# A hybrid encoder layer on one core: how the group norms, the mixer's table splits and the gate products are put in order

## The chip, the cores and the metric

The kernel runs on one core of one Trainium2 chip. The metric is the device time of one execution in microseconds (us). Engines: PE (TensorE, matmuls; its weight loads are shown as PEld), DVE (VectorE), ACT (ScalarE), POOL (GpSimd), and SP, which here only issues DMAs. Every engine works through its own queue in a fixed order that is set when the kernel is built; engines wait for each other by semaphores.

## The reference: what is computed

One encoder layer over 512 tokens of 1024 channels, in float32, batch 1:

- n = RMSNorm(x). z = n W_in with W_in 1024x2048, cut into four parts of 512 channels: `x_lru`, `g_lru`, `a_glu`, `b_glu`.
- Recurrent half: a causal-like convolution of 4 taps over `x_lru`, two gated linear recurrences (forward and backward; gates by block-diagonal 64x64 matrices and sigmoids), their sum times gelu(`g_lru`).
- Convolution half: `a_glu` x sigmoid(`b_glu`), a depthwise convolution of 31 taps, a layer norm over groups of 64 channels, SiLU.
- Both halves are RMS-normed, joined and projected by W_out (1024x1024); h = x + that.
- PEER: queries RMSNorm(h) W_q; for each token and 8 heads the best 16 of 128x128 experts by product keys (two rankings of 128, then a ranking of sums), a softmax over the 16 as gates; each expert is a row of `peer_u` and a row of `peer_v`: out = sum of gate x gelu(u . n) x v. h = h + out, and a last RMSNorm.

## The kernel before

Matmul operands are split into a high and a low part in a rounded format (`split`: the cast to `w_hi` on ACT, L108, and the subtraction to `w_lo` on an engine given by the caller, L110); each product is three matmuls (high x high, high x low, low x high). Activations have their parts in `m_hi` and `m_lo`.

The program runs through five stages: the mixer (0 to 276 us), ranking with the queries (to about 500), the scatter of the gates into a table in memory, `scr_g` (to about 670), then the dense experts: for tokens 0 to 383 all 128 tiles of 128 experts are computed densely, while the last 128 tokens gather their rows by indirect DMA (`gather_steps`, L691 and L701 on DVE); and a short end.

*The mixer.* Four token blocks are normed (`normed`: Square on ACT L130, `rstd_of` with a Sqrt at L120, L132 on DVE) and transposed (`turn`, L140 to L142). Then a loop goes over the 16 column blocks of W_in in the order `order`; n is the turn, eb the block. A turn splits its own block (subtraction on POOL), issues the load of the block two turns ahead, and runs 24 matmuls of 512 columns (L329 to L331) into a bank `pz`. What a turn hangs on to that: a gelu, a sigmoid or the gated product; the 31-tap convolutions `convs` (of channel groups 1 and 2 on DVE, L228; of groups 0 and 3 the first 8 taps on ACT and POOL, L220 and L221, and the other 23 as matmuls with diagonal tables, `taps`, L242 to L244, whose tables are split on POOL too); the recurrences `recur(0)` at n = 9 and `recur(2)` at n = 11 (gate matmuls L265 and L267, activations L270 to L280, products and scans on DVE L285 to L294, and L288, t = 1 - t, on ACT).

The group norm of channel group j is `gnorm(j)`: a matmul for the means (L304), subtraction (L305, DVE), Square (L307, ACT), a matmul per token block for the variances (L310), `rstd_of` (five small DVE instructions and a Sqrt), transposes (L314), a copy (L316, ACT), a matmul that spreads the factors (L318), the product (L319, DVE), SiLU (L320, ACT). `gnorm(1)` is called whole in turn n = 10. After the loop come the rest of the diagonal taps of group 3, `gnorm(0)`, `gnorm(2)`, `halves(0)`, `gnorm(3)`, `project(0)` and `project(1)`. `halves(hf)` makes the two parts of four channel groups and the RMS factor `ry` of that half (Squares L389, sums on POOL L391, a matmul L400); `project(hf)` multiplies by W_out (L417 to L419) into the three `pz` banks, eight groups of 12 matmuls, and a bank is emptied by a DVE instruction that needs `ry` (L420).

*The dense experts.* `dense_u(i)` gives tile i the gelu of its scores in a buffer w (24 matmuls of 384 columns, L464 to L466); 51 tiles are made ahead (`AHEAD_U`). `weigh(i, w)` multiplies by the gates (L730, DVE), casts (L732, ACT) and subtracts (L734, DVE); `dense_v` runs 18 matmuls of 512 columns into `po` (L758). The gates come from `scr_g` in groups of 8 tiles, 1.5 MB a load (`load_gates`, L726), into two buffers `g_s`. Turn i of the last loop weighs tile i + 2 and multiplies tile i.

*What sets the order.* The framework orders each engine's instructions when the kernel is built, by the order of the program text as priority and by a model of when operands are ready; an instruction whose operands the model has ready can be put ahead of older ones. `with tc.issue_after(ins)` keeps the instructions of the block that run on the engine of `ins` behind `ins` in that engine's queue; it adds no semaphore.

Of the kernel before, what the change touches and what calls it, by code (L numbers as in the profile page):

```python
# [8 lines left out]
F32 = mybir.dt.float32  # L9
# [4 lines left out]
AF = mybir.ActivationFunctionType  # L14
ALU = mybir.AluOpType
# [3 lines left out]
P = 128  # L19
# [41 lines left out]
def tile_kernel(ctx, tc, x, par, wi, bd, kd, mg, wo, wq, keys, u_rows, v_rows, u_t, v_t, fg, ffg, sel, out):  # L61
    nc = tc.nc
# [35 lines left out]
    def f(t):  # L98
        return t.bitcast(F32)

    def load(src):
        t = raw.tile([P, D], F32, name="raw_t")
        nc.sync.dma_start(t, src)
        return t

    def split(t, eng, pool=wp):
        hi = pool.tile([P, D], F32R, name="w_hi")
        nc.scalar.copy(hi, t)  # L108
        lo = pool.tile([P, D], F32R, name="w_lo")
        eng.tensor_sub(lo, t, f(hi))  # L110
        return hi, lo

    def flat(t):
        return t.rearrange("p a b -> p (a b)")

    def rstd_of(pool, ss, n, tags=("r_v", "r_s", "r_r", "r_q")):

        v, s, r, q = (pool.tile(list(ss.shape), F32, name=t) for t in tags)
        nc.vector.tensor_scalar(v, ss, 1.0 / n, EPS, op0=ALU.mult, op1=ALU.add)
        nc.scalar.activation(s, v, AF.Sqrt)  # L120
        nc.vector.reciprocal(r, s)
        nc.vector.tensor_mul(q, r, r)
        nc.vector.tensor_mul(q, q, v)
        nc.vector.tensor_scalar(q, q, -0.5, 1.5, op0=ALU.mult, op1=ALU.add)
        nc.vector.tensor_mul(r, r, q)
        return r
# [18 lines left out]
    with ExitStack() as mx:  # L145
# [11 lines left out]
        with ExitStack() as m1:  # L157
# [8 lines left out]
            xc = a2.tile([P, 4, T], F32, name="xc", bufs=1)  # L166
            xls = [a2.tile([P, T + 3], F32, name=f"xl{i}", bufs=1) for i in range(2)]

            xt = [load(x[b * P:(b + 1) * P, :]) for b in range(2)]
            mgb = a2.tile([P, D], F32, name="mgb", bufs=1)  # L170
            nc.sync.dma_start(mgb, mg.partition_broadcast(P))
            xt += [load(x[b * P:(b + 1) * P, :]) for b in range(2, NB)]
            wts = {eb: load(wi[eb].rearrange("p c e -> p (c e)")) for eb in order[:AHEAD]}
            nc.sync.dma_start(pr, par)
            nc.sync.dma_start(sl, sel)
            nc.sync.dma_start(flat(bdt.rearrange("p a b c d -> p (a b c) d")), bd)
            nc.sync.dma_start(ffb, ffg.partition_broadcast(P))
            for xl in xls:
                nc.vector.memset(xl[:, 0:2], 0.0)
                nc.vector.memset(xl[:, T + 2:T + 3], 0.0)  # L180
# [72 lines left out]
            def advance(g, n):  # L253
                for _ in range(n):
                    next(g, None)
# [3 lines left out]
            def recur(j0):  # L259

                rs_, is_, ts_, qs_ = {}, {}, {}, {}
                for j in (j0, j0 + 1):
                    for d in range(2):
                        g_r = ps_t.tile([P, T], F32, name="pt")
                        nc.tensor.matmul(g_r, bdt[:, d, 0, j, :], xc[:, j, :], start=True, stop=True)  # L265
                        g_i = ps_t.tile([P, T], F32, name="pt")
                        nc.tensor.matmul(g_i, bdt[:, d, 1, j, :], xc[:, j, :], start=True, stop=True)  # L267
                        q = d * 4 + j
                        r = rs_[q] = a2.tile([P, T], F32, name="r")
                        nc.scalar.activation(r, g_r, AF.Sigmoid, bias=pc("brg", q))  # L270
                        ig = is_[q] = a2.tile([P, T], F32, name="ig")
                        nc.scalar.activation(ig, g_i, AF.Sigmoid, bias=pc("big", q))
                        t = ts_[q] = a2.tile([P, T], F32, name="t")
                        nc.scalar.activation(t, r, AF.Tanh, scale=lm[:, q:q + 1])
                        nc.gpsimd.tensor_mul(ig, ig, xc[:, j, :])
                for q, r in rs_.items():
                    nc.scalar.activation(r, r, AF.Exp, scale=lm2[:, q:q + 1])
                for q, t in ts_.items():
                    s = qs_[q] = a2.tile([P, T], F32, name="sq")
                    nc.scalar.activation(s, t, AF.Sqrt)  # L280
                for j in (j0, j0 + 1):
                    for d in range(2):
                        q = d * 4 + j
                        e, t, s = rs_[q], ts_[q], qs_[q]
                        nc.vector.scalar_tensor_tensor(t, e, 1.0, t, op0=ALU.add, op1=ALU.mult)  # L285
                        nc.vector.scalar_tensor_tensor(s, e, 1.0, s, op0=ALU.add, op1=ALU.mult)
                        nc.vector.tensor_mul(s, s, is_[q])
                        nc.scalar.activation(t, t, AF.Copy, scale=-1.0, bias=1.0)  # L288
                        if d == 0:
                            nc.vector.tensor_tensor_scan(hs[:, j, :], t, s, 0.0, op0=ALU.mult, op1=ALU.add)  # L290
                        else:
                            nc.vector.tensor_tensor_scan(e[:, ::-1], t[:, ::-1], s[:, ::-1], 0.0,
                                                         op0=ALU.mult, op1=ALU.add)
                            nc.vector.tensor_add(hs[:, j, :], hs[:, j, :], e)  # L294
# [3 lines left out]
            selg = sl[:, P:P + 2]  # L298
            bcg = sl[0:2, P + 2:SELN]

            def gnorm(j):
                cv = y[:, 4 + j, :]
                pb = ps_t.tile([P, T], F32, name="pt")
                nc.tensor.matmul(pb, ones64, cv, start=True, stop=True)  # L304
                nc.vector.scalar_tensor_tensor(cv, pb, -1.0 / 64.0, cv, op0=ALU.mult, op1=ALU.add)  # L305
                s = tmp.tile([P, T], F32, name="s2", bufs=3)
                nc.scalar.activation(s, cv, AF.Square)  # L307
                pv = ps_t.tile([P, T], F32, name="pt")
                for b in range(NB):
                    nc.tensor.matmul(pv[:, 2 * b:2 * b + 2], s[:, b * P:(b + 1) * P], selg, start=(b == 0), stop=(b == NB - 1))  # L310
                r = rstd_of(tmp, pv[:, 0:2 * NB], 64, ("g_v", "g_s", "g_r", "g_q"))
                pr_ = ps_t.tile([P, T], F32, name="pt")
                for b in range(NB):
                    nc.tensor.transpose(pr_[0:2, b * P:(b + 1) * P], r[:, 2 * b:2 * b + 2], ident)  # L314
                rs = tmp.tile([2, T], F32, name="rs", bufs=2)
                nc.scalar.copy(rs, pr_[0:2, :])  # L316
                pb = ps_t.tile([P, T], F32, name="pt")
                nc.tensor.matmul(pb, bcg, rs, start=True, stop=True)  # L318
                nc.vector.tensor_mul(cv, cv, pb)  # L319
                nc.scalar.activation(cv, cv, AF.Silu, scale=pc("ng", j), bias=pc("nb", j))  # L320

            for n, eb in enumerate(order):
                hi, lo = split(wts.pop(eb), nc.gpsimd)
                if n + AHEAD < len(order):
                    wts[order[n + AHEAD]] = load(wi[order[n + AHEAD]].rearrange("p c e -> p (c e)"))
                pz = ps_z.tile([P, T], F32, name="pz")
                for c in range(NC):
                    cs = slice(c * P, (c + 1) * P)
                    nc.tensor.matmul(pz, hi[:, cs], m_hi[:, c, :], start=(c == 0), stop=False)  # L329
                    nc.tensor.matmul(pz, hi[:, cs], m_lo[:, c, :], start=False, stop=False)  # L330
                    z_end = nc.tensor.matmul(pz, lo[:, cs], m_hi[:, c, :], start=False, stop=(c == NC - 1))  # L331
                kind, j = divmod(eb, 4)
                if kind == 0:
                    xl = xls[j % 2]
# [24 lines left out]
                if 1 <= n <= 4:  # L359
                    advance(convs[1], 8)  # L360
                if n >= 5:
                    advance(convs[2], {5: 7}.get(n, 4) if n < 10 or n > 12 else 0)
                if n >= 6:
                    advance(convs[0], 2)
                if n >= 12:
# [2 lines left out]
                    advance(taps[0], 1)  # L368
                if kind == 1:
                    nc.vector.tensor_mul(hs[:, j, :], hs[:, j, :], gg[:, j, :])  # L370
                if n == 10:
                    with tc.issue_after(z_end.ins):
                        gnorm(1)

            m2 = mx.enter_context(ExitStack())
            wp2 = m2.enter_context(tc.tile_pool(name="wp2", bufs=4))
# [52 lines left out]
            with tc.issue_after(z_end.ins):  # L429
                advance(taps[1], 100)  # L430
                for g in convs:
                    advance(g, 100)
                gnorm(0)
                gnorm(2)
                ry = halves(0)
                gnorm(3)
                project(0, ry)
                project(1, halves(1))
            m2.close()
# [280 lines left out]
    def gates_of(i):  # L720
        n, o = divmod(i, GQ)
        return gbuf[n][:, :, o * GT:(o + 1) * GT]

    def load_gates(n):
        t = gq.tile([P, NT, GQ * GT], F32, name="g_s")
        nc.sync.dma_start(t, scr_g[:, :, n * GQ * GT:(n + 1) * GQ * GT].rearrange("a p s -> p a s"))  # L726
        gbuf[n] = t

    def weigh(i, w):
        nc.vector.tensor_mul(w, w, gates_of(i))  # L730
        whi = gq.tile([P, TD], F32R, name="wt_hi", bufs=LAST)
        nc.scalar.copy(whi, flat(w))  # L732
        wlo = gq.tile([P, TD], F32R, name="wt_lo", bufs=LAST)
        return whi, wlo, nc.vector.tensor_sub(wlo, flat(w), f(whi))  # L734

    gq = ctx.enter_context(tc.tile_pool(name="gq", bufs=2, side="right"))
    acc = gq.tile([P, D], F32, name="acc", bufs=1)
# [136 lines left out]
```

## Time and profile before

| | |
|---|---|
| median of 3 runs | 1566.47 us (1563.59 to 1568.61) |
| the profiled execution | 1564.53 us, its span 1562.8 us |
| PE busy | 94% of the span |
| DVE busy | 79% |
| ACT busy | 41% |
| POOL busy | 42% |
| mean granted PE clock | 0.97 |
| memory traffic | 229 GB/s over the span |

PE's share counts a matmul as busy from its start to a modelled end, and consecutive matmuls overlap; so 100% of a stretch can still hold a slower pace, and the number of matmuls in a stretch says more. The granted clock is 1.0 at 2.4 GHz and 0.5 at 1.2 GHz. Idle time of an engine costs only where the chain of waits runs through it.

### The profile page before, as it was taken

The page shows a single profiled execution, that of the slowest core. Times are in us where ns is not written, and L with a number is a line of the kernel's source. Part 1 is how long each engine was busy: PE and PEld are TensorE (multiplying, and loading weights), DVE is VectorE, ACT ScalarE, POOL GpSimd, SP SyncE. Part 2 cuts the span into 40 slices and gives each one's busy share as a digit, 9 for nine tenths or more (in the row PEclk, how much of TensorE's full clock was granted, in tenths as well). Part 3 has the DMA queues.
Part 4 walks back from the last instruction along what each step waited for, and adds up shares of the span by engine and source line. Part 5 has one row for each costly group of instructions (what it writes and reads, how often), then busy time and mean ns, then how long its engine had stood idle before and what let it go on. Part 6 is the DMA issues. An engine that isn't in the chain of part 4 may idle for free.

```text
span 1562.8 us, 21636 instructions
## 1 busy us (share of the span) xinstructions
PE 1475.6 (94%) x7939; PEld 1294.8 (83%) x7939; DVE 1230.5 (79%) x2255; ACT 636.4 (41%) x937; POOL 653.0 (42%) x382
## 2 busy tenths in 40 slices
PE   5987889999988999999899999999999999999997
PEld 4764657899977889898799999999999999888886
DVE  6995745599999999948777787777777877777776
ACT  5458443344434554442233333333333333333333
POOL 3644722476551000144455555445444444444440
PEclk9998879999989999999899999999999999999999
DMA  6220412323223666589999899998989988777783
GB/s 235 87 75 14 174 42 96 114 101 103 88 96 113 224 209 230 209 254 368 334 325 344 295 340 302 334 325 301 347 300 345 320 308 308 284 276 275 263 290 134
DMA packets 137787, 358.69 MB, mean 230 GB/s; under 512 B 10064, under 2 KB 59472, under 8 KB 134352
## 3 DMA queue, kind: packets, MB, share of 16 engines
q1 hardware_dynamic: 100240, 222.03, 41.8%
q0 software_dynamic: 36864, 134.23, 23.4%
q8 instruction: 62, 1.02, 0.3%
q10 hardware_dynamic: 576, 1.05, 0.2%
q14 instruction: 45, 0.37, 0.1%
HBM read 327.91 MB, written 29.36 MB: 229 GB/s over the span
## 4 chain that ended last, share of the span: by engine, by line
PE 77%; DVE 15%; DMA 3%; ACT 2%; issue 2%; POOL 1%; SPq 0%; DVEq 0%; ACTq 0%; POOLq 0%
PE po L758 32%; PE p_e L464 10%; PE p_e L466 10%; PE p_e L465 10%; PE p_g L657 3%; DVE oa L651 2%; DMA g_s<-scr_g 2%; PE pq L573 2%; PE pq L575 2%; PE pq L574 2%; DVE w_lo L110 1%; DVE hot L647 1%; DVE pc L228 1%; PE pz L417 1%; PE pz L331 1%
## 5 line engine op out<-in xcount | busy, mean ns | idle before, releaser
L108 ACT CAST w_hi<-raw_t 128x1024 fp32r<-128x1024 f32 x302 | 316.0, 1050 | 399.0 <-PE p_e L465 255.1
L464 PE MATMUL p_e<-m_hi,w_hi 128*128 128x384 f32 x1024 | 352.6, 344 | 6.5 <-ACT w_e L473 5.7
L466 PE MATMUL p_e<-m_hi,w_lo 128*128 128x384 f32 x1024 | 349.8, 342 | 6.5 <-DVE w_lo L110 6.4
L465 PE MATMUL p_e<-m_lo,w_hi 128*128 128x384 f32 x1024 | 348.6, 340 | 0.3 <-DVE m_lo L142 0.3
L110 POOL TENSOR_TENSOR w_lo<-raw_t,w_hi 128x1024 fp32r<-128x1024 f32 x74 | 199.0, 2703 | 344.3 <-ACT w_hi L108 331.2
L679 POOL DMA_INDIRECT g_t<-in_u_rows,eidx x128 | 210.7, 1646 | 215.4 <-DVE g_t L691 175.3
L110 DVE TENSOR_TENSOR w_lo<-raw_t,w_hi 128x1024 fp32r<-128x1024 f32 x228 | 275.3, 1219 | 12.0 <-ACT w_hi L108 11.9
L679 POOL DMA_INDIRECT g_t<-in_v_rows,eidx x128 | 189.3, 1479 | 224.8 <-DVE acc L701 213.4
L758 PE MATMUL po<-w_hi,wt_hi 128*128 128x512 f32 x768 | 240.6, 393 | 0.0
L758 PE MATMUL po<-w_hi,wt_lo 128*128 128x512 f32 x768 | 239.4, 391 | 0.0
L758 PE MATMUL po<-w_lo,wt_hi 128*128 128x512 f32 x768 | 238.8, 390 | 0.0
L464 PEld LDWEIGHTS p_e<-m_hi,w_hi 128*128 128x128 f32 x1024 | 196.3, 192 | 10.9 <-ACT w_e L473 6.4
L466 PEld LDWEIGHTS p_e<-m_hi,w_lo 128*128 128x128 f32 x1024 | 195.8, 191 | 7.9 <-DVE w_lo L110 7.9
L465 PEld LDWEIGHTS p_e<-m_lo,w_hi 128*128 128x128 f32 x1024 | 195.9, 191 | 3.5 <-DVE m_lo L142 0.5
L758 PEld LDWEIGHTS po<-w_lo,wt_hi 128*128 128x128 f32 x768 | 144.1, 188 | 33.3 <-DVE w_lo L110 0.3
L758 PEld LDWEIGHTS po<-w_hi,wt_lo 128*128 128x128 f32 x768 | 144.3, 188 | 30.4
L691 DVE SCALAR_TENSOR_TENSOR g_t<-g_t,Xg 128x1024 f32<-128x1024 f32 x128 | 151.8, 1222 | 17.2 <-DMA g_t<-in_u_rows,eidx 17.2
L758 PEld LDWEIGHTS po<-w_hi,wt_hi 128*128 128x128 f32 x768 | 143.1, 188 | 25.0 <-ACT w_hi L108 0.2
L701 DVE SCALAR_TENSOR_TENSOR acc<-g_t,dots,acc 128x1024 f32<-128x1024 f32 x127 | 162.4, 1278 | 1.0 <-DMA g_t<-in_v_rows,eidx 1.0
L732 ACT CAST wt_hi<-w_f 128x384 fp32r<-128x384 f32 x69 | 35.4, 513 | 183.0 <-PE po L758 183.0
L734 DVE TENSOR_TENSOR wt_lo<-w_f,wt_hi 128x384 fp32r<-128x384 f32 x69 | 38.5, 558 | 88.6 <-ACT wt_hi L732 88.4
L651 DVE TENSOR_TENSOR oa<-hot,trb 128x1024 bf16<-128x1024 bf16 x144 | 92.2, 697 | 0.6
(220 smaller groups left out, 1911.8 us busy)
## 6 DMA issues: line engine op xcount, KB each, us to landing
raw_t<-in_u_t SPq DMA_DIRECT2D x128, 512.0 KB, 5.8
raw_t<-in_v_t SPq DMA_DIRECT2D x128, 512.0 KB, 5.3
scr_g<-stg SPq DMA_DIRECT2D x24, 1024.0 KB, 4.8
g_s<-scr_g SPq DMA_DIRECT2D x16, 1536.0 KB, 12.9
raw_t<-in_wi SPq DMA_DIRECT2D x16, 512.0 KB, 3.9
raw_t<-in_wq SPq DMA_DIRECT2D x16, 512.0 KB, 3.8
raw_t<-in_wo SPq DMA_DIRECT2D x8, 512.0 KB, 3.7
raw_t<-in_kd SPq DMA_DIRECT2D x6, 512.0 KB, 3.6
```

The lines of the kernel that those rows point to most:

```text
L108: nc.scalar.copy(hi, t)
L110: eng.tensor_sub(lo, t, f(hi))
L464: nc.tensor.matmul(p, hi[:, cs], m_hi[:, c, :TD], start=(c == 0), stop=False)
L465: nc.tensor.matmul(p, hi[:, cs], m_lo[:, c, :TD], start=False, stop=False)
L466: nc.tensor.matmul(p, lo[:, cs], m_hi[:, c, :TD], start=False, stop=(c == NC - 1))
L651: nc.vector.tensor_tensor(oa[:, q], hot[:, 1], over(2 + q, 1), op=ALU.mult)
L657: nc.tensor.matmul(p[:, t, :], hot[:, 0, g, :, o], oa[:, q, g, :, o], start=(q == 0), stop=(q == 2))
L679: nc.gpsimd.indirect_dma_start(out=t, out_offset=None, in_=rows, in_offset=bass.IndirectOffsetOnAxis(ap=eidx[:, k // K, k % K:k % K + 1], ...
L691: nc.vector.scalar_tensor_tensor(t, t, 1.0, Xg, op0=ALU.mult, op1=ALU.mult, accum_out=dots[:, k:k + 1])
L701: nc.vector.scalar_tensor_tensor(acc, t, dots[:, k:k + 1], acc, op0=ALU.mult, op1=ALU.add)
L734: return whi, wlo, nc.vector.tensor_sub(wlo, flat(w), f(whi))
L758: nc.tensor.matmul(po[b][hf], lhs[:, bs], rhs[:, hf * 512:(hf + 1) * 512], start=(i == 0 and n == 0), stop=(i == NK - 1 and n == 2))
```

## The change

1. Start: an activation with Sqrt on one column (`warm`) is put ahead of everything on ACT. The loads of `sel` (selection tables of the group norms), `bd` (gate matrices) and `ffg` (a gain) leave the start: the first two are issued in turn 1, the third in turn 8.
2. `gnorm` becomes a generator, `gnorm_steps`, cut at three places into four phases: means, subtraction and Square; variances and factors; transposes and copy; spreading, product and SiLU. One phase is advanced in each turn, of group 1 from turn 10, of group 2 from turn 12, of group 0 from turn 13, behind the last matmul of that turn's block on PE. After the loop the rest of these runs, then `halves(0)`, then group 3's four phases, then the projections.
3. Each turn uses a split made in the turn before and then splits the next block. Blocks of turns 0, 1, 12 and 13 are subtracted on DVE, the others on POOL as before.
4. t = 1 - t (L288) moves from ACT to DVE as a `tensor_scalar`.
5. The convolution of group 2 is advanced by four taps in turns 10 to 12 too.
6. `weigh`: the gate product of a tile is queued on DVE behind the subtraction (L734) of the tile weighed two before it.

```diff
+            warm = sm.tile([P, 1], F32, name="warm")
+            nc.scalar.activation(warm, eps_[:, 0:1], AF.Sqrt)
 ...
-            nc.sync.dma_start(sl, sel)
-            nc.sync.dma_start(flat(bdt.rearrange("p a b c d -> p (a b c) d")), bd)
-            nc.sync.dma_start(ffb, ffg.partition_broadcast(P))
 ...
-                        nc.scalar.activation(t, t, AF.Copy, scale=-1.0, bias=1.0)
+                        nc.vector.tensor_scalar(t, t, -1.0, 1.0, op0=ALU.mult, op1=ALU.add)
 ...
-            def gnorm(j):
+            def gnorm_steps(j):
                 cv = y[:, 4 + j, :]
                 pb = ps_t.tile([P, T], F32, name="pt")
                 nc.tensor.matmul(pb, ones64, cv, start=True, stop=True)
                 nc.vector.scalar_tensor_tensor(cv, pb, -1.0 / 64.0, cv, op0=ALU.mult, op1=ALU.add)
                 s = tmp.tile([P, T], F32, name="s2", bufs=3)
                 nc.scalar.activation(s, cv, AF.Square)
+                yield
                 pv = ps_t.tile([P, T], F32, name="pt")
 ...
                 r = rstd_of(tmp, pv[:, 0:2 * NB], 64, ("g_v", "g_s", "g_r", "g_q"))
+                yield
 ...
                 nc.scalar.copy(rs, pr_[0:2, :])
+                yield
 ...
+            gn = [gnorm_steps(j) for j in range(4)]
+            nxt = split(wts.pop(order[0]), nc.vector)
             for n, eb in enumerate(order):
-                hi, lo = split(wts.pop(eb), nc.gpsimd)
+                hi, lo = nxt
                 if n + AHEAD < len(order):
                     wts[order[n + AHEAD]] = load(wi[order[n + AHEAD]].rearrange("p c e -> p (c e)"))
+                if n == 1:
+                    nc.sync.dma_start(flat(bdt.rearrange("p a b c d -> p (a b c) d")), bd)
+                    nc.sync.dma_start(sl, sel)
+                if n == 8:
+                    nc.sync.dma_start(ffb, ffg.partition_broadcast(P))
 ...
+                if n + 1 < len(order):
+                    nxt = split(wts.pop(order[n + 1]), nc.vector if n + 1 in (1, 12, 13) else nc.gpsimd)
 ...
-                    advance(convs[2], {5: 7}.get(n, 4) if n < 10 or n > 12 else 0)
+                    advance(convs[2], {5: 7}.get(n, 4))
 ...
-                if n == 10:
-                    with tc.issue_after(z_end.ins):
-                        gnorm(1)
+                with tc.issue_after(z_end.ins):
+                    for j, n0 in ((1, 10), (2, 12), (0, 13)):
+                        if n >= n0:
+                            advance(gn[j], 1)
 ...
-                gnorm(0)
-                gnorm(2)
+                for j in (1, 2, 0):
+                    advance(gn[j], 4)
                 ry = halves(0)
-                gnorm(3)
+                advance(gn[3], 4)
 ...
+    weighed = []
     def weigh(i, w):
-        nc.vector.tensor_mul(w, w, gates_of(i))
+        with tc.issue_after(weighed[-2].ins) if len(weighed) > 1 else ExitStack():
+            nc.vector.tensor_mul(w, w, gates_of(i))
         whi = gq.tile([P, TD], F32R, name="wt_hi", bufs=LAST)
         nc.scalar.copy(whi, flat(w))
         wlo = gq.tile([P, TD], F32R, name="wt_lo", bufs=LAST)
-        return whi, wlo, nc.vector.tensor_sub(wlo, flat(w), f(whi))
+        weighed.append(nc.vector.tensor_sub(wlo, flat(w), f(whi)))
+        return whi, wlo, weighed[-1]
```

## Rows read from the trace of the kernel before

**Rows 1.** The page: PE's busy tenths in 40 slices of 39 us

```profile
PE   5987889999988999999899999999999999999997
```

**Rows 2.** Windows by stage: engines' busy us (count), granted clock, DMA share, GB/s

```profile
50.00:100.00 50.00, 48.32 (x199) 36.92 (x198) 47.81 (x60) 27.91 (x40) 33.44 (x18) 1.00 0.25 85
100.00:150.00 50.00, 38.71 (x144) 27.00 (x142) 31.07 (x39) 36.49 (x52) 18.24 (x10) 0.90 0.09 32
150.00:200.00 50.00, 38.80 (x150) 29.92 (x151) 36.95 (x30) 23.22 (x30) 37.50 (x16) 0.83 0.43 157
760.00:1360.00 600.00, 600.00 (x3023) 546.59 (x3022) 468.98 (x606) 212.11 (x290) 295.64 (x195) 1.00 0.91 319
```

**Rows 3.** Timeline of PE, mixer loop: start, us, instruction [idle before, releaser]

```profile
118.83 1.87 PE L310 MATMUL pt<-sl,s 128*128 128x2 f32 x8 [6.99 <-ACT s L307]
...
154.68 0.79 PE L329 MATMUL pz<-m_hi,w_hi 128*128 128x512 f32 x1 [7.86 <-ACT w_hi L108]
...
159.10 0.79 PE L331 MATMUL pz<-m_hi,w_lo 128*128 128x512 f32 x1 [3.20 <-POOL w_lo L110]
...
166.49 0.39 PE L331 MATMUL pz<-m_hi,w_lo 128*128 128x512 f32 x1
...
171.93 0.39 PE L331 MATMUL pz<-m_hi,w_lo 128*128 128x512 f32 x1
```

**Rows 4.** Timeline of PE, ACT and DVE around the first projection

```profile
188.32 1.02 PE L304 MATMUL pt<-y,sl 128*128 128x512 f32 x2
...
192.29 0.80 PE L418 MATMUL pz<-w_lo,m_hi 128*128 128x512 f32 x1 [2.72 <-POOL w_lo L110]
...
211.08 0.62 ACT L389 ACTIVATE s<-y 128x512 f32<-128x512 f32 x1
...
218.45 0.16 DVE L125 TENSOR_TENSOR r_r<-r_r,r_q 128x4 f32<-128x4 f32 x1
...
221.31 0.80 PE L417 MATMUL pz<-w_hi,m_hi 128*128 128x512 f32 x1 [0.93 <-DVE h_t L420]
...
239.34 0.75 DVE L420 SCALAR_TENSOR_TENSOR h_t<-pz,r_r,h_t 128x512 f32<-128x512 f32 x1 [2.04 <-PE pz L419]
```

**Rows 5.** Windows, line L417 alone: PE and PEld busy us, granted clock, DMA

```profile
210.00:221.00 11.00, 0.00 (x0) 0.00 (x0) 0.50 0.00 0
```

**Rows 6.** Timeline beside a POOL split; line L336 (ns min/median/max); groups of the page

```profile
103.16 0.69 DVE L286 SCALAR_TENSOR_TENSOR sq<-r,sq 128x512 f32<-128x512 f32 x1
...
108.04 6.00 POOL L110 TENSOR_TENSOR w_lo<-raw_t,w_hi 128x1024 fp32r<-128x1024 f32 x2 [12.41 <-ACT w_hi L108]
109.02 2.82 DVE L286 SCALAR_TENSOR_TENSOR sq<-r,sq 128x512 f32<-128x512 f32 x1
...
L336 DVE TENSOR_SCALAR xc<-xl,pr x4: 541/1228/1968, 64.8 to 93.9; 128x512 f32<-128x512 f32 x4
...
L110 DVE TENSOR_TENSOR w_lo<-raw_t,w_hi 128x1024 fp32r<-128x1024 f32 x228 | 275.3, 1219 | 12.0 <-ACT w_hi L108 11.9
```

**Rows 7.** Timeline of ACT and PE at the start

```profile
6.78 1.28 ACT L120 ACT_TABLE_LOAD   x1
8.08 0.29 ACT L120 ACTIVATE r_s<-r_v 128x1 f32<-128x1 f32 x2
...
20.29 3.65 PE L140 MATMUL pt<-ident,y 128*128 128x128 f32 x16 [5.91 <-DVE y L132]
```

**Rows 8.** Gate loads and waits (us, times, longest), 684 to 770 us; one window

```profile
748.00 1.11 SPq L726 DMA_DIRECT2D g_s<-scr_g  x1
...
g_s<-scr_g SPq DMA_DIRECT2D x16, 1536.0 KB, 12.9
...
DVE w_f L730 <- DMA g_s<-scr_g: 10.0, 3, 6.4
...
PE p_e L466 <- DVE w_lo L110: 6.4, 3, 3.0
...
750.00:760.00 10.00, 4.68 (x17) 3.34 (x17) 7.08 (x11) 2.78 (x4) 3.66 (x2) 0.75 1.13 335
```

## The prediction, made before the run

> **What bounds the kernel now.** I read the page's slices first. PE is at 9 tenths in every slice from the 21st to the 39th, but mostly at 5 to 8 in the first six, which are the mixer [rows 1]. The stage windows, read next, say how much that is worth: from 760 to 1360 us PE is busy in all 600 us at full clock, so nothing taken from another engine shortens that stage; between 100 and 200 us it is busy in 77.5 of 100 us, at a granted clock of 0.90 and then 0.83 [rows 2]. So time can be gained in the mixer and around the start of the dense experts, and each us gained there moves all that follows. The timeline of PE, third, names three holes of the mixer's loop: 6.99 us before the variance matmuls of `gnorm(1)`, which wait for their Square on ACT; 7.86 and then 3.20 us in one block's first matmuls, which wait for that block's split [rows 3]. The fourth hole is the largest: no matmul of the first projection runs from 210 to 221 us [rows 5], since its three banks are full and can't be emptied before `ry` at 218.45, and the last Square that `ry` needs runs on ACT at 211.08, behind two group norms that were put ahead of it [rows 4]. DVE is the second bound: busy in 47.81 of the 50 us from 50 to 100 [rows 2].
>
> **The change, part by part.** The sum is made against the profiled execution, 1564.5 us (span 1562.8), which is 2 us under the median of the runs; I add 2 at the end.
>
> *Start.* The Sqrt ahead of all takes the table load of 1.28 us at 6.78 off the path from x to the first transposes: ACT is idle before x lands. The subtractions of blocks 0 and 1 go from POOL to DVE at 1.22 us each [rows 6]. On DVE they can queue before the products of token blocks 2 and 3, for which PE waits 5.91 us [rows 7], or behind them; the POOL subtractions that hold DVE up in this stretch go. Bounds: 2.4 us lost less 1.3 (a loss of 1.1), to 1.3 plus most of the 5.9 (a gain of 6). I take a gain of 3, in the middle, as both engines' rows bear on it. Three loads leave SP's queue here and join it in turns 1 and 8; each costs an issue of under 1 us beside a queue that mostly waits for free buffers, and the tables are first read 60 us after turn 1: nothing, unless a gate matrix came late, which would show at once as a wait of L265.
>
> *The Trainium skill on the first term.* The table load lasts 1.28 us and the Sqrt starts 0.02 us behind it, so the row prices a switch at 1.30 [rows 7]. The page "ScalarE: Activation LUTs" (What ACT_TABLE_LOAD costs) puts a switch at about 2.66 us, a drain included; by it the start would gain 1.4 us more, and each new switch that the phases cause would cost twice as much. The row shows no such drain, and it decides.
>
> *The loop's holes.* With phases, PE runs the next block, 5.44 us [rows 3], between the means and the variances, so ACT and DVE have that long for the subtraction and the Square. With the split a turn ahead, the block's cast on ACT stands before that turn's gelu and taps instead of behind them, and in turn 13 DVE subtracts, idle then. So 6.99 + 7.86 + 3.20 = 18 us of waits are open to it. The half clock that follows such holes goes with them: a clock of 0.90 and 0.83 over two times 50 us is half clock in 10 + 17 = 27 us; some 21 of them are holes, and in the other 6 half the pace is lost: 3 us. Together 21. Against it, groups 2 and 0 now do their PE steps in the loop: one step takes about 1.0 us (L304 1.02, rows 4), four steps I estimate at 3.5 us, two groups at 7. Net 14. The limits: 21 if the extra steps lie in time that PE would have idled anyway, and nothing if DVE is what the loop waits for (a rival).
>
> *What queues behind the phases.* A phase's matmuls stand in PE's queue behind the block's last matmul, so if a Square, a factor or a copy is late, the next block is queued behind it on PE. On ACT the Sqrt and SiLU of a phase stand among gelu, sigmoid and tanh and can add a switch or two each, 1.3 us apiece. ACT has room (36.5 of 50 us, rows 2). I put 4 us for late phases over the loop, between 0 and the case worked out as a rival.
>
> *t = 1 - t on DVE.* Eight instructions. The nearest row is a `tensor_scalar` of the same shape, L336: 0.54 to 1.97 us, median 1.23 [rows 6]; so 4 to 16 us of DVE, I take 10. Half lies in the first recurrence, where DVE is full; but four round trips to ACT go, and POOL holds DVE less with four splits fewer. I cost it at nothing and keep +5 for the range. Group 2's taps in turns 10 to 12 cost nothing: as many as before, in another turn of the text.
>
> *The first projection.* From 188.32, when group 0's means start, to 239.34, its last emptying [rows 4]: 51 us. In it are 96 matmuls at 5.44 / 24 = 0.227, 21.8 us. After the change groups 0 and 2 are done before, the Squares of `halves(0)` wait for no group norm, and `ry` is there before the banks fill. What remains beside the 21.8: group 3's steps 3.5, the sum for `ry` 1, the first wait for POOL's splits of W_out 2.7 [rows 4], still there, and 2 for clock and emptying: 31. A gain of 20. The chain of group 3 is late next: its dozen dependent steps must fit beside the 22 us of matmuls. If they don't, some 8 us come back; if POOL's splits are early, 2 more are won.
>
> *The gates.* L730 runs far ahead now: 8 of 16 loads of 1.5 MB are issued by 748 us (the last of them is shown), when PE has used some 8 tiles, one group. DVE stands at a product whose gates are still under way, 10.0 us in three waits, and the split of v or u is queued behind it: PE waits 6.4 us for those, and from 750 to 760 it runs 17 matmuls in 4.68 us [rows 8]. At the pace of 760 to 1360 [rows 2] that window would hold 50. With the product behind the subtraction two tiles back, loads come once per 8 tiles, 5 of them (each 12.9 us to land) leave this stretch, and DVE's waits with them. Nothing is added on DVE; its products move to later, where it is busy in 469 of 600 us. Worth 6.4 us of waits plus about 2 of half clock: 8. The ends: 12, all that PE lacks here against its full pace, and -6, if later loads delay those of v and u (DMA share 0.91, rows 2).
>
> Sum: 3 + 14 - 4 + 20 + 8 = 41, so 1523.5 for the profiled execution, 1525 on the median's level.
>
> **Rivals.** (a) *DVE is the loop's bound.* A DVE product takes 0.69 us, and 2.82 beside a POOL split [rows 6]. If DVE, full from 50 to 100 us, stays full to the loop's end, the holes on PE close only as far as DVE's own time shrinks. Then the loop gains 0 and the projection 17: 3 + 0 + 17 + 8 = 28, so 1538. For it: 47.81 of 50. Against it: DVE is busy in only 31 of the 50 us from 100 to 150 [rows 2]. The Trainium skill, "SBUF — State Buffer" (Who interferes with whom), says that a DVE instruction with two SBUF inputs and a GpSimd instruction that reads SBUF block each other fully; the 2.82 beside the 0.69 agrees. (b) *The gates' order gives nothing:* the products were early because the tiles lay ready, and PE waits for u and v anyhow: 41 - 8 = 33, 1533. (c) *All holes go at no price:* 6 + 21 + 22 + 12 = 61, 1505. (d) *Slower.* Three groups put nine dependent phase steps into PE's queue in the loop, each behind DVE and ACT. If each waits as the one shown, 6.99 us [rows 3], that is 63, less the 7 there now: 56 lost, against 3 + 20 + 8 won and 11 from the split: 14 slower, 1580. It decides from (42 + 7) / 9 = 5.4 us a step on. Against it: a block of 5.44 us now lies between two steps.
>
> **How the numbers follow.** Forecast 1525 (its own range 1511 to 1540) 0.50; (a) 0.20, (b) 0.10, (c) 0.12, (d) 0.05; no change, all gains eaten by new waits, 0.03. The range 1500 to 1550 leaves out (d), no change, and edges of (a) and (c). Faster by over 0.3% (about what these runs can tell from no change): 0.50 + 0.20 + 0.10 + 0.12 = 0.92; same 0.03; slower 0.05.
>
> **What would show it.** Right: the last L420 of the first projection some 35 us earlier; no hole of over 3 us before L310, L329 or L331; ACT's L389 of `halves(0)` before group 3's chain; gate loads 66 us apart from the first third on, PE at full pace from 700 us. Wrong: PE waits at L310, L314 or L318 inside the loop (d), DVE full to the loop's end (a), or waits at L466 as before (b).

## The result, and the profile after

The changed kernel takes 1543.52 us (median of four runs, 1543.25 to 1544.67); the kernel before took 1566.65 in the same session (1563.59 to 1568.61). The ratio is 0.9856, with a 95% interval of 0.9838 to 0.9873: 23 us faster, where 41 were forecast. That lies in the range of 1500 to 1550, but outside of the forecast's own 1511 to 1540; the nearest of the times worked out is rival (a)'s 1538. The profiled execution has a span of 1541.5 us.

Line numbers are those of each run's own kernel. Five moments, in us from the start of the span, show where the 21 us between the two spans arose:

| | first z product | first product of the first projection | its last bank's emptying | first po product | last po product |
|---|---|---|---|---|---|
| before | 23.8 | 188.8 | 239.3 | 688.8 | 1552.8 |
| after | 24.7 | 199.6 | 232.0 | 682.7 | 1531.7 |
| the stretch up to it | 0.9 lost | 9.9 lost | 18.1 won | 1.2 lost | 15.0 won |

So the first projection paid nearly what was forecast (20) and the dense experts more (8), while the loop, which was to gain 10 us, lost that much. PE's work in the loop (columns as in [rows 2]), the kernel before, then after:

```profile
23.77:188.78 165.01, 144.17 (x573) 109.74 (x573) 131.43 (x155) 92.56 (x125) 90.66 (x45) 0.93 0.24 86
```

```profile
24.66:199.60 174.94, 153.89 (x615) 114.63 (x613) 135.56 (x177) 96.10 (x131) 97.47 (x47) 0.93 0.25 87
```

PE is idle for 20.8 us in the one and for 21.1 in the other: the old holes were exchanged for new ones. The 9.9 us lost are 9.7 of busy time, 42 matmuls more, most of them the group norms' steps that were moved here. The granted clock is the same. The page's slices [rows 1] and the windows [rows 2] of the kernel after:

```profile
PE   5998698999988999999999999999999999999997
```

```profile
50.00:100.00 50.00, 45.87 (x176) 34.74 (x175) 45.87 (x59) 21.09 (x31) 32.45 (x18) 0.93 0.25 84
100.00:150.00 50.00, 45.57 (x177) 33.01 (x176) 42.20 (x53) 38.07 (x54) 23.95 (x13) 0.97 0.13 43
150.00:200.00 50.00, 37.51 (x158) 26.15 (x157) 33.32 (x42) 30.15 (x39) 33.15 (x16) 0.90 0.35 125
760.00:1360.00 600.00, 600.00 (x3019) 544.37 (x3018) 470.10 (x600) 214.06 (x292) 293.01 (x195) 1.00 0.91 321
```

PE lost 2.5 us from 50 to 100 us, gained 7 from 100 to 150, and lost 1.3 again in the next 50. The holes of [rows 3] are gone but for one, and a new one is there. PE's waits up to 290 us (who waited, for whom, us in total, times, longest), those that are over 2 us in the loop; L242's was 1.7 before, and 3.6 of L316's 16.1 lie in the first projection:

```profile
PE pt L316 <- DVE g_r L125: 16.1, 3, 11.6
...
PE pc L242 <- DVE y L228: 4.1, 1, 4.1
PE pz L341 <- POOL w_lo L110: 3.7, 1, 3.7
```

```profile
166.83 1.01 PE L316 MATMUL pt<-ident,g_r 128*2 128x128 f32 x4 [11.58 <-DVE g_r L125]
```

L316 is the third phase of `gnorm(1)`: it transposes `g_r`, the factor that DVE computes in five small instructions. In the kernel before the same step, L314, waited 0.8 us in the loop. The timeline of DVE says why it is late now (start, us, instruction, idle before it):

```profile
134.16 0.69 DVE L285 SCALAR_TENSOR_TENSOR t<-r,t 128x512 f32<-128x512 f32 x1 [6.63 <-ACT sq L280]
...
144.62 2.83 DVE L287 TENSOR_TENSOR sq<-sq,ig 128x512 f32<-128x512 f32 x1
147.38 1.50 DVE L288 TENSOR_SCALAR t<-t 128x512 f32<-128x512 f32 x1
148.79 1.77 DVE L285 SCALAR_TENSOR_TENSOR t<-r,t 128x512 f32<-128x512 f32 x1
150.48 3.42 DVE L290 TENSOR_TENSOR_SCAN y<-t,sq 128x512 f32<-128x512 f32 x1
...
159.62 0.19 DVE L121 RECIPROCAL g_r<-g_s 128x8 f32<-128x8 f32 x1
...
166.53 0.15 DVE L125 TENSOR_TENSOR g_r<-g_r,g_q 128x8 f32<-128x8 f32 x1
```

`recur(2)`'s products start at 134.16, 12.8 us earlier than the 147.00 of before: here the change did what it should. But they take 31.1 us (24.7 in the kernel before, where POOL ran beside the second half of them too): POOL's taps and splits are beside them, 19.8 of 20 us busy from 140 to 160. L287 takes 2.83 us where it took 0.68 at 138.96, and the five instructions of `g_r` are queued among them. DVE stands still for less than 0.2 us between 134 and 168. Behind L316, in PE's queue, stand products that need nothing of this.

### The profile page after: what moved, and what is told of

It is laid out like the page before. It is cut to its first block, busy times and chain, and to the rows that moved or that the text cites. A ratio compares the mean times of both kernels' runs of the same rounds, so it can differ in the third digit from the quotient of the medians.

```text
span 1541.5 us, 21654 instructions
## 1 busy us (share of the span) xinstructions
PE 1467.7 (95%) x7939; PEld 1289.4 (84%) x7939; DVE 1232.5 (80%) x2267; ACT 626.7 (41%) x926; POOL 625.4 (41%) x378
## 4 chain that ended last, share of the span: by engine, by line
PE 81%; DVE 13%; ACT 3%; issue 1%; POOL 1%; DMA 0%; SPq 0%; DVEq 0%; ACTq 0%; POOLq 0%
PE po L777 34%; PE p_e L478 10%; PE p_e L479 10%; PE p_e L480 10%; PE p_g L671 3%; DVE oa L665 2%; PE pq L587 2%; PE pq L588 2%; PE pq L589 2%; DVE hot L661 1%; PE pz L432 1%; PE pz L431 1%; PE pz L433 1%; PE pz L339 1%; PE pz L340 1%
## 5 line engine op out<-in xcount | busy, mean ns | idle before, releaser
L110 POOL TENSOR_TENSOR w_lo<-raw_t,w_hi 128x1024 fp32r<-128x1024 f32 x70 | 189.8, 2720 | 349.2 <-ACT w_hi L108 349.2
L110 DVE TENSOR_TENSOR w_lo<-raw_t,w_hi 128x1024 fp32r<-128x1024 f32 x232 | 280.9, 1222 | 13.6 <-ACT w_hi L108 13.4
L693 POOL DMA_INDIRECT g_t<-in_u_rows,eidx x128 | 197.4, 1543 | 214.0 <-DVE g_t L705 170.2
L693 POOL DMA_INDIRECT g_t<-in_v_rows,eidx x128 | 178.7, 1396 | 234.8 <-DVE acc L715 222.1
```

The lines of the kernel that those rows point to most:

```text
L693: nc.gpsimd.indirect_dma_start(out=t, out_offset=None, in_=rows, in_offset=bass.IndirectOffsetOnAxis(ap=eidx[:, k // K, k % K:k % K + 1], ...
```

## The experiments

All ran against the kernel before in sessions where that took 1565.2 to 1566.4 us; the interval is that of the ratio to it (the changed kernel: 0.9838 to 0.9873). The theory at the outset: the gates gave 15 us; the loop lost because DVE's queue, not PE's, orders it.

**Run 1, the gates' order undone** (`e1_mixer_only`).

```diff
-        with tc.issue_after(weighed[-2].ins) if len(weighed) > 1 else ExitStack():
-            nc.vector.tensor_mul(w, w, gates_of(i))
+        nc.vector.tensor_mul(w, w, gates_of(i))
```

Expected: 

> The changed kernel without the gates' ordering: each gate product is queued as before, the rest of the change stays. In the changed kernel 21 us were gained between the first po product and the last, against 6.1 before the first. If the ordering is what gave the gates' part (theory: 15 us, the distance from the first po product to the last, 864.0 before and 849.0 after), the time returns to about 1558 us, PE has the two holes at 748 to 760 us of [rows 8] again and few matmuls at 740 to 760. If the ordering gave only the 8 us of the two holes and the rest came from an earlier start of the ranking, about 1551. If nothing: 1543.

Measured: 1557.96 us, 0.9937 to 0.9964. So this edit alone is worth 14.4 us, and the mixer the rest. The window from 680 to 780 us holds 429 matmuls here and 500 in the changed kernel; at the latter's 0.2 us each the 71 missing are 14.2 us. The two holes are back:

```profile
745.58 0.56 DVE L747 TENSOR_TENSOR w_f<-w_f,g_s 128x384 f32<-128x384 f32 x1 [6.37 <-DMA g_s<-scr_g]
```

```profile
747.65 0.44 PE L478 MATMUL p_e<-m_hi,w_hi 128*128 128x384 f32 x1 [2.24 <-ACT w_e L487]
...
751.70 0.69 PE L480 MATMUL p_e<-m_hi,w_lo 128*128 128x384 f32 x1 [3.43 <-DVE w_lo L110]
```

L747 is the gate product. Behind it on DVE stand the subtraction that ACT's gelu (L487) waits for and, after three products of the gathers (1.22 us each), the splits of v and u (L110).

**Run 2, the gates' loads crowded again, the order kept** (`e12_crowd`, the last to run).

```diff
 ...
+        if 6 <= i <= 10:
+            gs = slice((i - 1) * GQ * GT, i * GQ * GT)
+            nc.sync.dma_start(scr_x[:, :, gs], scr_g[:, :, gs])
```

Expected: 

> The changed kernel with five extra copies of 1.5 MB, from one memory tensor to another in the gate loads' small pieces, issued near the start of the dense down projection, where the kernel before had five gate loads more. The gates' ordering of DVE stays. Theory of order (what cost 14.4 us was DVE standing at a product whose gates were under way, with the split of v or u queued behind it): no product waits for these copies, PE stays at some 20 of 20 us from 700 to 760, and the time is 1543 to 1546. Theory of crowding (the loads themselves held up those of v and u): PE waits for the splits of v and u again, and the time is 1550 to 1558.

Measured: 1558.70 us, 0.9941 to 0.9969. The time is just above what the theory of crowding gave. No product waits for these copies, and yet all the gain is gone. ACT waits for u and v, and PE for ACT. Timelines of this kernel:

```profile
678.52 9.06 SPq L104 DMA_DIRECT2D raw_t<-in_v_t  x1
...
719.05 10.44 SPq L104 DMA_DIRECT2D raw_t<-in_u_t  x1
```

```profile
726.72 1.04 ACT L109 CAST w_hi<-raw_t 128x1024 fp32r<-128x1024 f32 x1 [15.77 <-DMA raw_t<-in_u_t]
```

```profile
727.82 0.69 PE L479 MATMUL p_e<-m_hi,w_hi 128*128 128x384 f32 x1 [12.39 <-ACT w_hi L109]
```

An issue of 512 KB that lasts 0.33 us in a quiet stretch holds SP for 9 to 10 us. So crowding can cost 15 us by itself. That it is what cost them in the kernel before is not shown: from 680 to 780 us ACT waits for no load of u or v there, nor in run 1, and PE's waits run by way of DVE, which stands at products ([rows 8], run 1). The issues of u and v last up to 5.2 us in the kernel before between 680 and 760, and up to 2.7 in the changed one; how the loss divides between the two stays open, since the copies here move twice the bytes of a gate load and come closer together.

**Run 3, the start on POOL** (`e2_start_pool`): `nc.vector` back to `nc.gpsimd` for the splits of turns 0 and 1.

Expected: 

> The table blocks of the first two turns are subtracted on POOL again; turns 12 and 13 stay on DVE. Theory: in the changed kernel DVE runs two subtractions of 1.23 us ahead of the third and fourth token blocks' L132, so the first z product comes at 24.66 instead of some 22; with them on POOL it comes 2 to 2.5 us earlier, and the time falls to about 1541. Rival: POOL's subtractions stretch L132 beside them as in the kernel before, the first z product stays within 0.7 us of 24.66, and the time stays at 1543 to 1544.

Measured: 1543.38 us, 0.9846 to 0.9880: no difference, but not as either side had it. The first z product came at 26.7, later than with DVE. POOL's three splits (15.05 to 21.99) stretch the small instructions and both L132 beside them:

```profile
15.08 2.39 DVE L123 TENSOR_TENSOR r_q<-r_q,r_v 128x1 f32<-128x1 f32 x2
17.44 0.22 DVE L124 TENSOR_SCALAR r_q<-r_q 128x1 f32<-128x1 f32 x2
17.63 2.15 DVE L125 TENSOR_TENSOR r_r<-r_r,r_q 128x1 f32<-128x1 f32 x2
19.75 4.53 DVE L132 SCALAR_TENSOR_TENSOR y<-raw_t,r_r,mgb 128x1024 f32<-128x1024 f32 x2
```

**Run 4, the start's splits on DVE, behind that work** (`e9_start_dve`).

```diff
-            nxt = split(wts.pop(order[0]), nc.vector)
+            with tc.issue_after(scaled.ins):
+                nxt = split(wts.pop(order[0]), nc.vector)
```

`scaled` is L132 of the last token block; the splits of turns 1 and 2 are treated likewise.

Expected: 

> Only the start of the changed kernel is altered: the subtractions of turns 0 to 2 all run on DVE, queued behind L132 of the last token block, so that neither DVE's queue nor POOL stands in the way of that block. The first z product came at 23.8 us before, at 24.7 in the changed kernel, and at 26.7 with POOL alone. Theory: L132 of blocks 2 and 3 (4.53 us for two) takes 2.4 us and comes 2.5 us earlier, the first z product comes at 20 to 21 us; since conv's work on DVE waits for these products (10.07 us idle) and sets the end of the loop, the whole kernel is 3 to 4 us shorter: 1539.5 to 1541. Rival (the start is hidden behind DVE's later queue, as moving the subtractions to POOL changed nothing): 1543 to 1544.

Measured: 1536.11 us, 0.9799 to 0.9827: some 7 us won, more than expected. The two L132 take 2.48 us and are through by 18.0 instead of 22.6; the first z product comes at 20.8, as expected, and the first projection 5.5 us earlier. The conv's products on DVE start at 33.91 (38.04 in the changed kernel, 39.11 in run 3), and those of `recur(2)` at 128.91 (134.16 and 134.07). In run 3 and here DVE waits once less for ACT's copy (L348 of the changed kernel, where that wait is 1.86 us); this made up for run 3's delay and is a part of what was won here. So the start is on the path by way of DVE, but not every us of it counts.

**Run 5, a phase ahead of the recurrence** (`e3_phase_first`).

```diff
                 if n == 11:
+                    with tc.issue_after(z_end.ins):
+                        advance(gn[1], 1)
                     recur(2)
 ...
-                        if n >= n0:
+                        if n >= n0 and (n, j) != (11, 1):
```

Expected: 

> The second phase of the group norm gn[1] is issued ahead of recur(2) instead of behind it. Theory of order: the 11.58 us in which L316 waits for g_r are DVE's queue, in which the five instructions of g_r stand behind recur(2)'s products; ahead of them they are done by about 140 us, the hole goes, and the first projection begins 8 to 10 us earlier: 1534 to 1536. Theory of contention: the small instructions and the products are slow because POOL runs beside them, so what DVE does late stays late; a hole of 7 us or more stays, at L316 or at the next thing that needs DVE, and the time is 1541 to 1544. A wait of some 4 us at L311 may come in its place, which would give about 1538.

Measured: 1554.54 us, 0.9909 to 0.9936: 11 us slower, and both theories missed. `g_r` is ready at 130.1, as the theory of order had it. But the phase's Sqrt falls among `recur(2)`'s sigmoids on ACT, and PE waits 2.27 us for L307 with the gate matmuls queued behind:

```profile
127.55 1.28 ACT L120 ACT_TABLE_LOAD   x1
128.84 0.21 ACT L120 ACTIVATE g_s<-g_v 128x8 f32<-128x8 f32 x1
129.07 1.28 ACT L270 ACT_TABLE_LOAD   x1
```

The products start at 142.11 instead of 134.16, take as long as in the changed kernel (31.6 us), and the next group norm's subtraction (L305, at 172.49) is queued behind them on DVE; its Square on ACT, and PE, wait for it:

```profile
173.87 1.87 PE L311 MATMUL pt<-sl,s 128*128 128x2 f32 x8 [10.64 <-ACT s L307]
```

Here what delays the start of DVE's products delays all that follows.

**Runs 6 and 7, POOL taken off.** `e4_tail_dve` puts the splits of turns 14 and 15 and of the second tap tables on DVE; `e6_pool_quiet` also `conv(3)`'s taps:

```diff
+                if j == 3:
+                    nc.vector.tensor_scalar(cv, glu[:, j, 0:T], pc("kw", j * CK), pc("kb", j), op0=ALU.mult, op1=ALU.add)
+                    yield
+                    for k in range(1, CV):
+                        nc.vector.scalar_tensor_tensor(cv, glu[:, j, k:k + T], pc("kw", j * CK + k), cv, op0=ALU.mult, op1=ALU.add)
+                        yield
+                    return
 ...
```

Expected: 

> The subtractions of turns 14 and 15 and of the second to last tables of taps[1] are put from POOL to DVE, the order of everything else stays. Theory of contention: recur(2)'s products (1.5 to 3.4 us beside POOL, 0.4 to 0.7 alone) shrink, g_r is ready 6 to 8 us earlier although DVE has some five instructions of 1.22 us more, the hole of 11.58 us at L316 falls under 5, and the time is 1536 to 1538. Theory of order: the five instructions stay behind the products and behind the added subtractions, the hole stays above 9 us, and the time is 1543 to 1546.

Expected: 

> Like the run with the tail's subtractions on DVE, and conv[3]'s seven taps go from ACT and POOL to DVE as well (eight instructions of some 0.7 us, ahead of recur(2)'s products, where DVE stood idle 6.6 us), so POOL does nothing beside these products. Theory of contention: they take 14 to 16 us as recur(0)'s did, instead of 31, g_r is ready near 150 us instead of 166.7, and no wait over 5 us is left before the last z product; the time is 1531 to 1536. Theory of order: the products stay above 1 us each or the wait stays above 9 us behind DVE's longer queue, and the time is 1540 to 1546.

Measured: 1541.95 us (0.9841 to 0.9873) and 1541.71 us (0.9826 to 0.9855), 2 us at most. With POOL quiet (run 7) contention is gone: the products take 15 us instead of 31 (137.20 to 152.32). The time hardly moved all the same, since PE now waits for block 14's split, queued behind these products on DVE:

```profile
154.26 0.80 PE L348 MATMUL pz<-m_hi,w_lo 128*128 128x512 f32 x1 [10.56 <-DVE w_lo L110]
```

**Run 8, the phases later** (`e5_phase_late`).

```diff
-                    for j, n0 in ((1, 10), (2, 12), (0, 13)):
-                        if n >= n0:
+                    for j, ns in ((1, (10, 11, 14, 15)), (2, (12, 14, 15)), (0, (14, 15))):
+                        if n in ns:
```

Expected: 

> The third and fourth phases of the group norm gn[1], and the later ones of gn[2] and gn[0], are written two turns later, so that in PE's queue the rest of the table blocks' products stands ahead of the first L316 instead of behind it; DVE's work stays. Theory (DVE's queue is the bound from 134 to 168 us, and PE only needs other work in that time): PE fills the 11.58 us with some 30 block products (7 to 8 us), L316 finds g_r ready, the first projection begins about 8 us sooner and the time is 1535 to 1537. Rival (the first projection waits for what DVE finishes late anyway, so PE's filled hole opens again ahead of it): the last z product comes 8 us sooner, the first projection does not, and the time is 1541 to 1544.

Measured: 1538.03 us, 0.9803 to 0.9833: 5 us won, but not where the theory put them. L316 still waits 12.1 us and PE is busy 19.0 us from 134 to 168 (18.7 in the changed kernel). The last z product is no earlier (177.1). What went are the holes behind it: the first projection begins 2.2 us and ends 5.1 us earlier.

**Runs 9 and 10, both together** (`e7_late_quiet`, run 9: the edits of runs 7 and 8; `e8_late_conv`, run 10: the same, but all splits as in the changed kernel).

Expected: 

> Both edits together: POOL quiet beside recur(2), and the group norms' later phases behind the last blocks' products. If contention is what makes DVE late, the quiet POOL has taken most of the hole and the order adds 0 to 3 us: 1529 to 1534. If order and contention are two separate costs, the gains add up to 12 to 16 us: 1527 to 1531. If DVE's queue is the bound whatever is done, 1538 or more.

Expected: 

> The group norms' later phases behind the last blocks' products and conv[3]'s taps on DVE, but the last blocks' subtractions stay on POOL (1530.0 us with them on DVE, where the product of block 14 waits 10.3 us for a subtraction queued behind recur(2)). If the wait of 10.3 us is only that queue, POOL gives these parts by 144 to 148 us, the wait falls under 5 us, and the time is 1524 to 1529. If POOL's four subtractions beside recur(2) stretch its products again (15 us quiet, 31 beside both), DVE ends some 8 us later and the time is 1532 to 1537.

Measured: 1530.01 us (0.9762 to 0.9797) and 1531.78 us (0.9768 to 0.9796). Together the two edits win 13 us, more than 2 and 5: with DVE early, what the later phases leave free for PE can be used. Where the last splits run makes no difference: on DVE block 14 waits 10.3 us for its split, on POOL L323 (L316 in the changed kernel) waits 10.6 us for DVE's stretched products. One engine's lateness shows up in front of whichever dependent instruction PE meets first.

**Runs 11 and 12, DVE's queue in the order PE needs** (`e10_recur_halves`: run 9, with the products of `recur(2)`'s second block behind the splits of 14 and 15; `e11_all`: with run 4's start).

```diff
 ...
-                    recur(2)
+                    rec2 = recur(2)
+                    advance(rec2, 1)
+                if n == 14:
+                    advance(rec2, 2)
                     rec.close()
 ...
```

`recur` is a generator here that stops after each channel block.

Expected: 

> The quiet POOL with the late phases (1530.0 us), and recur(2)'s products of its second channel block are issued after the subtractions of blocks 14 and 15 instead of ahead of them. Theory: the wait of 10.3 us for block 14's subtraction falls under 3 us, since its input is ready at 139 us, and DVE's own work ends as before: the time falls by 5 to 9 us, to 1521 to 1525. Rival (DVE's sum sets the end, PE's hole only moves to the group norms or the first projection): 1528 to 1530.

Expected: 

> The halves of recur(2) and the altered start together. If both theories hold the gains add up: 1518 to 1522. If the start gains nothing it equals the run with the halves alone.

Measured: 1523.60 us (0.9725 to 0.9752) and 1518.49 us (0.9680 to 0.9707). The wait for block 14's split fell from 10.3 to 3.2 us. The windows of the three kernels after one another (the changed kernel, run 9, run 11; columns as in [rows 2]; the first starts and ends with DVE's full stretch):

```profile
134.00:168.00 34.00, 18.73 (x75) 14.60 (x74) 33.84 (x33) 15.47 (x24) 24.70 (x11) 0.84 0.19 61
```

```profile
134.00:168.00 34.00, 23.66 (x99) 18.39 (x98) 27.36 (x49) 13.88 (x22) 0.89 (x1) 0.85 0.32 124
```

```profile
134.00:168.00 34.00, 30.25 (x137) 22.93 (x136) 32.55 (x55) 22.02 (x31) 1.27 (x1) 1.00 0.34 124
```

DVE is nearly as busy in the last as in the first, but with 55 instructions instead of 33, and PE does 137 matmuls instead of 75. `e11_all` is 25 us faster than the changed kernel and 47 faster than the one before.

## Why the prediction was right, and where it was wrong

The time lies in the range and the direction is right, but only 21 of the 41 us came. Of the terms, the start and the loop failed, and the gates gave nearly twice their share. Without that surplus of 7 us, for which the term was mis-sized, the time would have been at the edge of the range: that it lies inside owes something to luck and to the width of the range.

- *Start, +3:* measured 0.9 lost. The table load's 1.3 us were won: the first transposes start at 9.32 us instead of 10.71. They were lost again before the first z product. The step that failed is the choice of the middle between "ahead of" and "behind" the products of token blocks 2 and 3: the subtractions run ahead of both, and POOL's split of turn 2 beside them, so the two L132 take 4.53 us, and PE's wait of 5.91 [rows 7] is 6.24 now. Queued behind them (run 4) the first z product comes 3.0 us earlier than in the kernel before, which is the 3 of the term, and the first of the conv 2.2. DVE of the kernel after:

```profile
14.94 1.23 DVE L110 TENSOR_TENSOR w_lo<-raw_t,w_hi 128x1024 fp32r<-128x1024 f32 x1 [0.29 <-ACT w_hi L108]
...
18.02 4.53 DVE L132 SCALAR_TENSOR_TENSOR y<-raw_t,r_r,mgb 128x1024 f32<-128x1024 f32 x2
```

- *The loop's holes +14, late phases -4:* together +10, measured 9.9 lost. The holes of 6.99, 7.86 and 3.20 [rows 3] went but for one of 3.69, and busy time grew by 9.7 us with the added steps, where I took 7; the 3 us of half clock did not come back, since the granted clock of the loop stayed at 0.93. The failing step is the 4 us for late phases: L316 alone waits 12.5 in the loop, L242 2.4 more than before, and the sum of PE's idle time did not fall. I bounded it by ACT's table switches and saw that the next block queues behind a late factor, but priced no DVE queue behind `recur(2)`. Rival (a) has the mechanism: DVE is full, and PE's holes close only as far as DVE's time shrinks. It put the time at 1538 with the loop at 0. The evidence I held against it, 31 of 50 us from 100 to 150, was an average over idle time that DVE spent waiting for others (in the kernel before 10.34 us for PE up to 141.40 and 4.92 for ACT up to 147.00), and it stopped short of the stretch behind it that counts, 134 to 168 us of the kernel after.
- *t = 1 - t on DVE, 0:* six take 0.42 us and the two beside POOL 1.5, so 5.5 us where I took 10; not separated by a run.
- *First projection, +20:* 18.1. `r_r` is ready at 206.41 (218.45 in [rows 4]) and nine products of L431 run from 210 to 221 us, where none did [rows 5]:

```profile
210.00:221.00 11.00, 4.46 (x9) 2.14 (x9) 0.69 0.01 1
```

  What is missing is L316's last wait, 3.57 us at 210.23, and r_r's small instructions beside POOL's four splits of W_out (194.77 to 205.09), 2.31 us for one of 128x4.
- *The gates, +8:* 15.0. The direction was right, the term was too small: I priced 6.4 us of waits and the one window of [rows 8], where the shortfall runs from 700 to 760. The reason named first, DVE standing at a product, is what the waits of run 1 show; run 2 shows that loads in this stretch can cost as much without it. How much each gave is open. Columns as in [rows 8], the kernel before, then after:

```profile
700.00:760.00 60.00, 51.27 (x239) 44.79 (x238) 48.22 (x79) 17.30 (x23) 21.57 (x15) 0.93 1.10 360
```

```profile
700.00:760.00 60.00, 60.00 (x307) 54.81 (x306) 46.25 (x68) 21.07 (x29) 29.21 (x20) 1.00 0.91 321
```

Rival (b) is out by run 1, (c) by the new waits, and (d) had the right mechanism at one step of nine: L316's 11.58 is over its 5.4, the others in the loop wait under 1.

Of the signs of being right, ACT's Squares of `halves(0)` do come before group 3's chain, the gate loads are 63 to 68 us apart up to 1294 us, and PE has no hole from 700 to 760 us. But the first projection's last L420 came 7.3 us earlier and not 35, and a hole of 3.7 us stayed before L341, which is L331 of the kernel before. Two signs of being wrong showed: PE's wait at L316, which is L314 of the kernel before, for (d), and the full DVE for (a).

On contention the Trainium skill, "SBUF — State Buffer" (Who interferes with whom), says more than I drew from it: a `tensor_scalar` in a two-port mode is blocked as well, though it has one input. L288 fits that: 0.42 us alone, 1.50 beside POOL; that it ran in such a mode no run here shows. The conv's products, with one input in PSUM, keep their 0.75 us whatever POOL does, as the same page has it.

## What to carry to other kernels

An engine is the bound of a stretch when its queue, not its average, is full between two things that another engine needs: read its timeline from the first late instruction back to the first idle gap. Before a dependent step goes into a strict queue, look up what stands ahead of its input on the engine that makes it, and at what speed that runs beside its neighbours. Two edits that gain 2 and 5 us alone can be worth 13 together, as here, when one engine's lateness only moves from one waiting instruction to the next.

## What the runs showed of the hardware

- Small DVE instructions can be stretched by as many us as large ones beside POOL: 128x8 in 0.14 us alone (run 6) and 2.23 at 161.82 in the changed kernel, 128x4 in 2.31.
- A table switch on ACT costs 1.30 us also in mid-kernel (1.28 and 0.01 to 0.02 to the next instruction, run 5); two of them, among the sigmoids that DVE waits for, were part of a delay of 7.9 us.
- Bunched DMAs hold the issuing queue: among five copies of 1.5 MB from memory to memory, one issue of 512 KB on SP lasted 10.44 us instead of 0.33 (run 2).
